# A transfer-bound mixture of softmaxes: loads and stores trade issuing engines, and one early unit is weighed in pairs

## The chip, the core and the metric

The kernel runs on one core of one Trainium2 chip. The metric is the device time of one execution in microseconds (us). The core's compute engines here are VectorE (DVE in the profile), ScalarE (ACT) and GpSimd (POOL); SyncE (SP) only issues transfers. Transfers started by SyncE and by ScalarE go through two queues (q1 and q10 in the profile) onto the same 16 transfer engines. All times compared below are fast runs, unless it is said otherwise.

## The reference

```python
batch, seq, vocab, num_heads = 32, 128, 4096, 4      # float32
prior_probs = softmax(prior, axis=-1)                # over the 4 heads
softmax     = softmax(logits, axis=-1)               # over the vocabulary
mixture     = np.sum(prior_probs[..., None] * softmax, axis=2)
```

The inputs are 268 MB of logits, the output is 67 MB. Both must cross the transfer engines once.

## The kernel before

The 4096 rows are cut into 32 **units** (U = 32) of 128 rows. One unit has four heads of 4096 columns, 8.39 MB, loaded into one of two halves of `ltile`. ScalarE takes the exponential of each head and its sum; VectorE takes a reciprocal, GpSimd multiplies it by the prior, and VectorE adds up the four weighted heads into one of two halves of `obuf`, which is stored. `only(ins, *keep)` states all that an instruction waits for.

```python
def load(u):                                   # SyncE issues
    ...
    ld = nc.sync.dma_start(out=ltile[:, u % 2, h:to], in_=lg[u // J, u % J, :, h:to, :])
    if u >= 2:
        only(ld, adds[u - 2, 0] if h == 0 else exps[u - 2, to - 1])
...
with tc.manual_schedule():
    load(0)
    nc.scalar.dma_start(out=pr, in_=pv)        # the prior
    load(1)
    ...
    for u in range(U):
        ...
        free = (stores[u - 2],) if bufd and u >= 2 else ()
        m = H if u < U - 4 else 2              # heads weighed in groups of m
        for h in range(H):
            if h == 2 and 0 < u < U - 3:
                store(u - 1, obuf[:, (u - 1) % 2], nc.scalar)   # ScalarE issues
            exp(h, *(free if m == H and h == H - 1 else ()))
            if (h + 1) % m:
                continue
            mul = weigh(g, m, ...)             # reciprocal, times prior
            for k in range(g, h + 1):
                add(k, mul, ...)               # VectorE; k = 0 writes, k > 0 adds
        if u + 2 < U:
            load(u + 2)
        ...                                    # the last stores, on SyncE
```

`exp(h)` of unit u waits for its load and, for h > 0, for `adds[u - 1, h]`, because the exponentials share one set of buffers. The fourth also waits for the store of unit u-2, since the weighings that follow overwrite its half of `obuf`.

The softmax here doesn't subtract the row's maximum and nothing guards it: scores larger than these inputs give would overflow.

Of the kernel before, what the change touches and what calls it, by code (L numbers as in the profile page):

```python
# [35 lines left out]
@with_exitstack  # L36
def kernel(
    ctx: ExitStack,
    tc: tile.TileContext,
    logits: bass.AP,  # L40
    prior: bass.AP,
    out: bass.AP,
):
    nc = tc.nc
    nc.at_finalize(early_transfers)
    B, S, H, V = logits.shape
    assert prior.shape == (B, S, H)
    assert out.shape == (B, S, V)
    P = 128
    J = 2  # L50
    R = P * J
    G = B * S // R
    U = G * J
    assert G * R == B * S and G <= 32 and H == 4

    lg = logits.rearrange("b s h v -> (b s) h v").rearrange("(g p j) h v -> g j p h v", p=P, j=J)
    ov = out.rearrange("b s v -> (b s) v").rearrange("(g p j) v -> g j p v", p=P, j=J)
    pv = prior.rearrange("b s h -> (b s) h").rearrange("(g r) h -> g r h", r=R)

    cpool = ctx.enter_context(tc.tile_pool(name="cpool", bufs=1))  # L60
    psum = ctx.enter_context(tc.tile_pool(name="psum", bufs=1, space=bass.MemoryType.PSUM))



    before = {}

    def only(ins, *keep):
        for k in keep:
            tc.add_manual_dep(
                ins.ins,  # L70
                k.ins.name,
                mybir.DependencyInfo(mybir.DependencyClass.Sync, mybir.DependencyReason.DATA),
                reason="all that this instruction waits for",
            )
        tc.declare_no_dep(
            ins.ins,
            group="loop",
            keep=[k.ins for k in keep] + before.get(ins.ins.engine, []),
            reason="covered by the waits that are kept",
        )  # L80
        tc.add_to_no_dep_group("loop", ins.ins)
        before[ins.ins.engine] = [ins.ins]
        return ins


    ltile = cpool.tile([P, 2, H, V], FP32, name="ltile")
    loads = {}
    exps = {}
    adds = {}
    stores = {}  # L90

    def load(u):
        if u == 0 or u >= U - 3:
            cuts = (0, 2, 3, 4) if u == U - 1 else (0, 2, 4)
        else:
            cuts = (0, H)
        for h, to in zip(cuts, cuts[1:]):
            ld = nc.sync.dma_start(  # L98
                out=ltile[:, u % 2, h:to], in_=lg[u // J, u % J, :, h:to, :]
            )  # L100


            if u >= 2:
                only(ld, adds[u - 2, 0] if h == 0 else exps[u - 2, to - 1])
            else:
                only(ld)
            for k in range(h, to):
                loads[u, k] = ld

    def store(u, acc, eng, lo=0, hi=V):  # L110
        st = eng.dma_start(out=ov[u // J, u % J, :, lo:hi], in_=acc[:, lo:hi])  # L111
        stores[u] = only(st, adds[u, H - 1])


    pr = cpool.tile([G, R, H], FP32, name="pr")
    pn = cpool.tile([32, H, R], FP32, name="pn")
    pmax = cpool.tile([G, R], FP32, name="pmax")
    pp = cpool.tile([P, J, H, 32], FP32, name="pp")


    dsum = cpool.tile([P, U, H], FP32, name="dsum")
    rden = cpool.tile([P, U, H], FP32, name="rden")
    coeff = cpool.tile([P, U, H], FP32, name="coeff")



    ebuf1 = cpool.tile([P, V], FP32, name="ebuf1")
    ebuf2 = psum.tile([P, V], FP32, name="ebuf2")
    ebuf3 = cpool.tile([P, V], FP32, name="ebuf3")
    obuf = cpool.tile([P, 2, V], FP32, name="obuf")  # L130

    with tc.manual_schedule():
        load(0)
        nc.scalar.dma_start(out=pr, in_=pv)
        load(1)
        nc.gpsimd.memset(pn, 0.0)  # L136
        nc.vector.reduce_max(pmax, pr, axis=AX.X)  # L137
        nc.vector.tensor_sub(pr, pr, pmax.unsqueeze(2).to_broadcast([G, R, H]))  # L138
        nc.scalar.activation(pr, pr, AF.Exp)  # L139
        nc.vector.reduce_sum(pmax, pr, axis=AX.X)  # L140
        nc.vector.reciprocal(pmax, pmax)  # L141
        nc.vector.tensor_mul(  # L142
            pn[0:G].rearrange("g h r -> g r h"), pr, pmax.unsqueeze(2).to_broadcast([G, R, H])
        )
        pq = pn.rearrange("g h (p j) -> g j h p", j=J)
        for t in range(P // 32):
            nc.vector.transpose(pp[32 * t : 32 * (t + 1)], pq[:, :, :, 32 * t : 32 * (t + 1)])  # L147

        for u in range(U):
            bufd = u < U - 2  # L150
            lt = ltile[:, u % 2]
            acc = obuf[:, u % 2] if bufd else lt[:, 0]
            es = (lt[:, 0], ebuf1, ebuf2, ebuf3) if bufd else [lt[:, h] for h in range(H)]
            ppu = pp[:, u % J, :, u // J]

            def exp(h, *keep):
                ex = nc.scalar.activation(  # L157
                    es[h], lt[:, h], AF.Exp, accum_out=dsum[:, u, h : h + 1]
                )
                keep = (loads[u, h],) + keep  # L160
                if bufd and h and u:
                    keep += (adds[u - 1, h],)
                exps[u, h] = only(ex, *keep)

            def weigh(h, n, *keep):
                rc = nc.vector.reciprocal(rden[:, u, h : h + n], dsum[:, u, h : h + n])  # L166
                only(rc, exps[u, h + n - 1])
                mul = nc.gpsimd.tensor_mul(  # L168
                    coeff[:, u, h : h + n], rden[:, u, h : h + n], ppu[:, h : h + n]
                )  # L170
                return only(mul, rc, *keep)

            def add(h, mul, lo=0, hi=V):
                if h == 0:
                    st = nc.vector.tensor_scalar(  # L175
                        out=acc[:, lo:hi], in0=es[h][:, lo:hi], scalar1=coeff[:, u, h : h + 1],
                        scalar2=None, op0=ALU.mult,
                    )
                    adds[u, h] = only(st, mul)
                else:  # L180
                    st = nc.vector.scalar_tensor_tensor(  # L181
                        out=acc[:, lo:hi], in0=es[h][:, lo:hi], scalar=coeff[:, u, h : h + 1],
                        in1=acc[:, lo:hi], op0=ALU.mult, op1=ALU.add,
                    )
                    adds[u, h] = only(st, mul, adds[u, h - 1])



            free = (stores[u - 2],) if bufd and u >= 2 else ()

            m = H if u < U - 4 else 2
            for h in range(H):
                if h == 2 and 0 < u < U - 3:
                    store(u - 1, obuf[:, (u - 1) % 2], nc.scalar)
                exp(h, *(free if m == H and h == H - 1 else ()))
                if (h + 1) % m:
                    continue
                g = h + 1 - m
                mul = weigh(g, m, *(free if m < H and g == 0 else ()))
                for k in range(g, h + 1):  # L200
                    n = 2 if u == U - 1 and k == H - 1 else 1
                    w = V // n
                    for c in range(n):
                        add(k, mul, c * w, (c + 1) * w)
                        if n > 1:
                            store(u, acc, nc.sync, c * w, (c + 1) * w)
            if u + 2 < U:
                load(u + 2)
            if u == U - 3:
                store(u - 1, obuf[:, (u - 1) % 2], nc.sync)  # L210
                store(u, acc, nc.sync)
            elif u == U - 2:
                store(u, acc, nc.sync)


# [28 lines left out]
```

## Time and profile before

| | kernel before |
|---|---|
| time, median (6 runs) | 780.93 us (780.84 to 781.11) |
| span in the profile | 779.3 us |
| VectorE, ScalarE busy | 67%, 60% |
| mean rate over the span | 431 GB/s |
| rate from 210 to 600 us | 434 GB/s |
| period of one unit in the steady part | 24.17 us |

How the transfers look is shown in the prediction. One more view is needed: the timeline of the same stretch from one store issue to the next. Columns of a timeline are start, duration, engine, line, instruction; in brackets the idle time before it and what ended it. (L111 issues a store, L157 is an exponential, L166 to L181 are the weighing.)

```profile
72.70 0.34 ACTq L111 DMA_DIRECT2D out_dram<-obuf  x1
73.09 3.59 ACT L157 ACTIVATE ebuf<-ltile 128x4096 f32<-128x4096 f32 x1 [1.06 <-DVE obuf L181]
...
76.71 3.60 ACT L157 ACTIVATE ebuf<-ltile 128x4096 f32<-128x4096 f32 x1
...
80.43 0.18 DVE L166 RECIPROCAL rden<-dsum 128x4 f32<-128x4 f32 x1 [7.76 <-ACT ebuf L157]
80.69 0.20 POOL L168 TENSOR_TENSOR coeff<-rden,pp 128x4 f32<-128x4 f32 x1 [23.96 <-DVE rden L166]
80.92 2.35 DVE L175 TENSOR_SCALAR obuf<-ltile,coeff 128x4096 f32<-128x4096 f32 x1 [0.31 <-POOL coeff L168]
83.31 13.53 DVE L181 SCALAR_TENSOR_TENSOR obuf<-ebuf,coeff,obuf 128x4096 f32<-128x4096 f32 x3
```

Follow it as a ring: the store is issued at 72.70, the third and fourth exponentials follow, then reciprocal, prior, one weighing of 2.35 and three that take 13.53 together, which end at 96.84; the next store is issued at 96.86. The ring is 96.86 - 72.70 = **24.16 us** long, and the transfers need 24.17 us for a unit.

### The profile page before, as it was taken

How to read it: one execution, taken by the hardware profiler on the slowest of the kernel's cores; microseconds unless marked ns; L12 is line 12 of the kernel's file. 1: busy time of each engine (PE TensorE's matmuls, PEld its weight loads, DVE VectorE, ACT ScalarE, POOL GpSimd, SP SyncE). 2: the span in 40 equal slices, each digit the busy share in tenths (PEclk: the TensorE clock that was granted, in tenths of full speed). 3: DMA queues.
4: the chain of work that ended last, by engine and by line, in shares of the span. 5: the costliest groups of instructions: out<-in, count | busy, mean ns of one | idle time of the engine just before them, and what ended most of it. 6: DMA issues, size and time to landing. Idle time of an engine off the chain costs nothing.

```text
span 779.3 us, 628 instructions
## 1 busy us (share of the span) xinstructions
DVE 521.0 (67%) x174; ACT 470.0 (60%) x258; POOL 8.3 (1%) x41
## 2 busy tenths in 40 slices
DVE  4447865568655686556875558755587555788986
ACT  4476555765557655577555675556755567557782
POOL 0000000000000000000000000000000000000000
DMA  9999999999999999999999999999999999999998
GB/s 407 457 417 397 474 407 417 444 455 434 404 468 401 460 420 416 458 443 418 417 468 407 454 407 468 420 415 447 415 459 417 459 402 464 410 427 431 434 429 379
DMA packets 10117, 335.65 MB, mean 431 GB/s; under 512 B 1137, under 2 KB 1137, under 8 KB 1153
## 3 DMA queue, kind: packets, MB, share of 16 engines
q1 hardware_dynamic: 6048, 276.83, 82.3%
q10 hardware_dynamic: 4064, 58.79, 17.6%
q14 instruction: 5, 0.03, 0.0%
HBM read 268.50 MB, written 67.11 MB: 431 GB/s over the span
## 4 chain that ended last, share of the span: by engine, by line
DVE 55%; ACT 26%; DMA 15%; issue 2%; ACTq 1%; POOL 1%; DVEq 0%; SPq 0%; POOLq 0%
DVE obuf L181 45%; ACT ebuf L157 24%; DMA ltile<-in_logits_dram 9%; DVE obuf L175 8%; DMA out_dram<-obuf 6%; ACT ltile L157 1%; ACTq L111 1%; DVE ltile L181 1%; POOL coeff L168 1%; DVE rden L166 1%; DVEq L239 0%; SPq L98 0%; POOLq L239 0%; POOLq L168 0%
## 5 line engine op out<-in xcount | busy, mean ns | idle before, releaser
L181 DVE SCALAR_TENSOR_TENSOR obuf<-ebuf,coeff,obuf 128x4096 f32<-128x4096 f32 x90 | 403.6, 4484 | 3.8 <-POOL coeff L168 0.6
L157 ACT ACTIVATE ebuf<-ltile 128x4096 f32<-128x4096 f32 x90 | 323.7, 3597 | 39.6 <-DVE obuf L181 32.2
L157 ACT ACTIVATE ltile<-ltile 128x4096 f32<-128x4096 f32 x38 | 137.3, 3614 | 247.6 <-DMA ltile<-in_logits_dram 247.6
L166 DVE RECIPROCAL rden<-dsum 128x4 f32<-128x4 f32 (+1 forms) x36 | 6.3, 175 | 230.3 <-ACT ebuf L157 227.5
L175 DVE TENSOR_SCALAR obuf<-ltile,coeff 128x4096 f32<-128x4096 f32 x30 | 70.6, 2353 | 10.3 <-POOL coeff L168 10.3
L181 DVE SCALAR_TENSOR_TENSOR ltile<-ltile,coeff 128x4096 f32<-128x4096 f32 (+1 forms) x7 | 27.0, 3874 | 0.8 <-POOL coeff L168 0.6
L157 ACT ACTIVATION_READ_ACCUMULATOR ebuf<-ltile 128x1 f32 x90 | 16.8, 186 | 0.0
L168 POOL TENSOR_TENSOR coeff<-rden,pp 128x4 f32<-128x4 f32 (+1 forms) x36 | 7.2, 200 | 755.3 <-DVE rden L166 745.2
L157 ACT ACTIVATION_READ_ACCUMULATOR ltile<-ltile 128x1 f32 x38 | 7.1, 186 | 0.0
L175 DVE TENSOR_SCALAR ltile<-ltile,coeff 128x4096 f32<-128x4096 f32 x2 | 4.7, 2353 | 0.6 <-POOL coeff L168 0.6
L137 DVE TENSOR_REDUCE pmax<-pr 16x256 f32<-16x1024 f32 x1 | 1.2, 1206 | 5.4 <-DMA pr<-in_prior_dram 5.4
L139 ACT ACTIVATE pr<-pr 16x1024 f32<-16x1024 f32 x1 | 1.1, 1055 | 5.7 <-DVE pr L138 5.7
L142 DVE TENSOR_TENSOR pn<-pr,pmax 16x1024 f32<-16x1024 f32 x1 | 1.9, 1925 | 0.1
L140 DVE TENSOR_REDUCE pmax<-pr 16x256 f32<-16x1024 f32 x1 | 1.2, 1208 | 1.1 <-ACT pr L139 1.1
L139 ACT ACT_TABLE_LOAD x1 | 1.3, 1283 | 0.9 <-PEq L228 0.9
L147 DVE STREAM_TRANSPOSE pp<-pn 32x256 f32<-32x256 f32 x4 | 1.7, 436 | 0.1
L141 DVE RECIPROCAL pmax<-pmax 16x256 f32<-16x256 f32 x1 | 1.7, 1741 | 0.0
L138 DVE TENSOR_TENSOR pr<-pr,pmax 16x1024 f32<-16x1024 f32 x1 | 1.2, 1211 | 0.0
L136 POOL MEMSET pn<- 32x1024 f32 x1 | 0.9, 941 | 0.5 <-POOLq L228 0.5
L228 POOL MEMSET const-bfloat16-1.0<- 128x1 bf16 x1 | 0.1, 107 | 0.0
L228 POOL MEMSET const-uint8-127<- 128x1 uint8 x1 | 0.1, 107 | 0.0
L228 POOL MEMSET const-float32-0.0<- 128x1 f32 x1 | 0.1, 103 | 0.2 <-issue 0.2
(1 smaller groups left out, 0.1 us busy)
## 6 DMA issues: line engine op xcount, KB each, us to landing
out_dram<-obuf ACTq DMA_DIRECT2D x28, 2048.0 KB, 28.1
ltile<-in_logits_dram SPq DMA_DIRECT2D x7, 4096.0 KB, 25.5
ltile<-in_logits_dram SPq DMA_DIRECT2D x2, 2048.0 KB, 30.9
out_dram<-obuf SPq DMA_DIRECT2D x2, 2048.0 KB, 33.9
out_dram<-ltile SPq DMA_DIRECT2D x1, 2048.0 KB, 17.2
out_dram<-ltile SPq DMA_DIRECT2D x2, 1024.0 KB, 4.8
ltile<-in_logits_dram SPq DMA_DIRECT2D x28, 29.6
pr<-in_prior_dram ACTq DMA_DIRECT2D x1, 64.0 KB, 5.2
```

The costliest lines, as they stand in the source:

```text
L111: st = eng.dma_start(out=ov[u // J, u % J, :, lo:hi], in_=acc[:, lo:hi])
L137: nc.vector.reduce_max(pmax, pr, axis=AX.X)
L138: nc.vector.tensor_sub(pr, pr, pmax.unsqueeze(2).to_broadcast([G, R, H]))
L139: nc.scalar.activation(pr, pr, AF.Exp)
L141: nc.vector.reciprocal(pmax, pmax)
L142: nc.vector.tensor_mul(pn[0:G].rearrange("g h r -> g r h"), pr, pmax.unsqueeze(2).to_broadcast([G, R, H]))
L147: nc.vector.transpose(pp[32 * t : 32 * (t + 1)], pq[:, :, :, 32 * t : 32 * (t + 1)])
L157: ex = nc.scalar.activation(es[h], lt[:, h], AF.Exp, accum_out=dsum[:, u, h : h + 1])
L166: rc = nc.vector.reciprocal(rden[:, u, h : h + n], dsum[:, u, h : h + n])
L168: mul = nc.gpsimd.tensor_mul(coeff[:, u, h : h + n], rden[:, u, h : h + n], ppu[:, h : h + n])
L175: st = nc.vector.tensor_scalar(out=acc[:, lo:hi], in0=es[h][:, lo:hi], scalar1=coeff[:, u, h : h + 1], scalar2=None, op0=ALU.mult,)
L181: st = nc.vector.scalar_tensor_tensor(out=acc[:, lo:hi], in0=es[h][:, lo:hi], scalar=coeff[:, u, h : h + 1], in1=acc[:, lo:hi], op0=ALU.mu ...
```

## The change

It swaps the issuing engines, so that ScalarE, which runs its program in order, no longer stands at a store until VectorE has finished a unit, and weighs unit 1 in two pairs of heads, so that VectorE starts it earlier. The last four stores go behind the last loads on the loads' queue, as they did before.

```diff
-            ld = nc.sync.dma_start(
+            ld = nc.scalar.dma_start(
...
-        nc.scalar.dma_start(out=pr, in_=pv)
+        nc.sync.dma_start(out=pr, in_=pv)
...
-            m = H if u < U - 4 else 2
+            m = 2 if u == 1 or u >= U - 4 else H
             for h in range(H):
                 if h == 2 and 0 < u < U - 3:
-                    store(u - 1, obuf[:, (u - 1) % 2], nc.scalar)
+                    store(u - 1, obuf[:, (u - 1) % 2], nc.sync)
+                if h == 2 and u == U - 1:
+                    store(u - 1, ltile[:, (u - 1) % 2, 0], nc.scalar)
...
-                            store(u, acc, nc.sync, c * w, (c + 1) * w)
+                            store(u, acc, nc.scalar, c * w, (c + 1) * w)
...
-            if u == U - 3:
-                store(u - 1, obuf[:, (u - 1) % 2], nc.sync)
-                store(u, acc, nc.sync)
-            elif u == U - 2:
-                store(u, acc, nc.sync)
+            if u == U - 2:
+                for k in (u - 2, u - 1):
+                    store(k, obuf[:, k % 2], nc.scalar)
```

## The prediction

> **What bounds the kernel now.** I read the page from the DMA rows downward, because the kernel does almost no arithmetic per byte: it reads 268 MB and writes 67 MB.
>
> ```profile
> DVE 521.0 (67%) x174; ACT 470.0 (60%) x258; POOL 8.3 (1%) x41
> ...
> DMA  9999999999999999999999999999999999999998
> ...
> DMA packets 10117, 335.65 MB, mean 431 GB/s; under 512 B 1137, under 2 KB 1137, under 8 KB 1153
> ...
> q1 hardware_dynamic: 6048, 276.83, 82.3%
> q10 hardware_dynamic: 4064, 58.79, 17.6%
> ```
>
> VectorE and ScalarE are each idle for a third of the span or more, while the transfer engines are at nine tenths in every slice but the last, and the two queues' shares add up to 99.9%. Queue 1 is SyncE's (all loads plus the four last stores: 268.4 + 4 x 2.1 = 276.8 MB), queue 10 is ScalarE's (28 stores of 2.1 MB and the prior). The chain that ended last is not what decides here: it is 55% VectorE and 26% ScalarE, because the compute loop is tuned to be just as long as the transfers. So I went to the waits, to see whether compute waits for data or data for compute.
>
> ```profile
> ACT ltile L157 <- DMA ltile<-in_logits_dram: 247.6, 32, 12.0
> DVE rden L166 <- ACT ebuf L157: 227.5, 30, 13.9
> ACT ebuf L157 <- DVE obuf L181: 32.2, 26, 1.9
> ...
> POOL coeff L168 <- DMA out_dram<-obuf: 10.0, 1, 10.0
> ```
>
> ScalarE waits 247.6 us for loads, about 8 us in each unit; VectorE then waits for ScalarE. The third line is ScalarE standing at the issue of a store: it sits between the second and third exponential of a unit until VectorE has finished the unit before, 32.2 us over 26 units, 1.24 us each. Next the timeline of one steady unit and of the next one's start:
>
> ```profile
> 88.32 3.62 ACT L157 ACTIVATE ltile<-ltile 128x4096 f32<-128x4096 f32 x1 [7.92 <-DMA ltile<-in_logits_dram]
> ...
> 96.86 0.34 ACTq L111 DMA_DIRECT2D out_dram<-obuf  x1
> 97.25 3.59 ACT L157 ACTIVATE ebuf<-ltile 128x4096 f32<-128x4096 f32 x1 [1.62 <-DVE obuf L181]
> ...
> 105.08 2.35 DVE L175 TENSOR_SCALAR obuf<-ltile,coeff 128x4096 f32<-128x4096 f32 x1 [0.32 <-POOL coeff L168]
> ```
>
> Unit 3's data is there at 88.32, unit 4's (from the same timeline) at 112.49, so the period is 24.17 us, and it repeats to 0.03 us in most of the 26 units. A unit moves 8.39 MB in and 2.10 MB out, 10.49 MB in 24.17 us = 433.8 GB/s. With stores absent the same rate appears: unit 1's load of 8.39 MB filled 22.39 to 41.73, 19.34 us, 433.7 GB/s. The rate is therefore the same with one or two queues in use, and the bound is that rate. The 335.65 MB of the kernel at 433.8 GB/s are 773.7 us. The remaining 5.6 us of the 779.3 us span are ends: the first 4.19 MB landed at 12.67 us where the rate alone would give 9.7 (about 3.0 us), the last 1 MB store took 4.8 us where the rate gives 2.4 (2.4 us). Some 0.7 us more was lost where two periods, 160.85 to 209.94, took 49.09 instead of 48.34 us; what disturbed them I cannot see.
>
> **What the Trainium skill says.** "DMA: Bandwidth & Descriptors", section "Where 436 GB/s comes from", puts the ceiling of a core's 16 ports at 435.2 GB/s; the 433.8 of the trace agrees, so no order of transfers should raise the steady rate. The same page, "Issuing engines are not separate DMA queues", says that transfers started by any engine run on the same 16 engines and that spreading them saves only issue time; the equal rates above agree. Its section "Queues, rings and completion order" says each engine takes turns between queues packet by packet. The mean packets here are 276.83 MB / 6048 = 45.8 KB and 58.79 MB / 4064 = 14.5 KB, semaphore packets included, and one store takes 28.1 us from issue to landing, where 2.1 MB alone would take 4.8: agrees with a turn of one 64 KB row of a load and one 16 KB row of a store, eight of each per engine and unit. "Perfetto Trace Analysis", section "DMA Optimizations", suggests one issuing engine for inputs and one for outputs; the kernel before does that already for nearly all transfers, so the change is a swap of the two.
>
> **The change part by part.**
>
> *Loads move to ScalarE's queue.* One load per unit, so one issue of about 0.34 us (the row of the store issue) replaces one store issue of 0.34 us: net zero in the loop. What moves is the place. The load of unit u+2 now stands after the fourth exponential of unit u and waits for VectorE's first weighing (reciprocal 0.18, GpSimd 0.20, gaps 0.3, weighing 2.35: about 3.1 us). ScalarE stands there 3.1 us which it otherwise would spend waiting for the next load: that wait is 7.9 to 8.4 us per unit. Nothing of it is on the path. In the kernel before the load is issued at 105.08 + 2.35 = 107.43, 5.1 us ahead of 112.49, when the load ahead of it lands; starting up costs about 3 us (the first load above), so the queue does not run dry.
>
> *Stores move to SyncE.* ScalarE loses the 1.24 us wait per unit. The third exponential can then start at about L + 7.3 instead of L + 8.9 (L is the landing of the unit). The fourth waits for the store of unit u-2 to land. In the kernel before that is exactly balanced: store issued 72.70, plus 28.1 is 100.8; the fourth exponential starts at 100.86. So most of the 1.6 us would merely turn into a wait for this store unless it lands earlier.
>
> *Unit 1 in pairs* is what makes it land earlier. VectorE is free at 46.14 and could start unit 1 after its second exponential (49.04) and not at 56.76. Two weighings (2.35 + 4.50) end at about 56.4, two more (9.0) at about 65.9, so store 1 is issued at 65.9 and not at 72.70, while store 0 is still moving (46.17 + 28.1 = 74.3). The store queue never goes empty, stores run some 2 us earlier from there on, and the fourth exponential is free again. Load 3 is issued at 56.2 instead of 59.1. All this is slack: the transfer engines are full either way. It could absorb part of the 0.7 us of disturbed periods: I count -0.4 us.
>
> *The tail.* The four last stores stood behind the last loads before as well; only the queue's name changes. Stores 28 and 29 now come after unit 30's exponentials (about 747) and not at 728 and 737, but the load of unit 31 keeps the queue busy till about 759. From 749.28, when the first pair of unit 31 has landed, two lengths must be compared. Transfers: 4.2 MB of loads and 8.4 MB of stores, 12.6 MB / 433.8 = 29.0 us. Compute: four exponentials to 763.79, then VectorE from 764.35 for 9.13 us, then 4.8 us for the last store: 778.3, also 29.0 us. ScalarE now issues store 30 between unit 31's second and third exponential; in the steady loop such an issue delays the next exponential by 0.39 us (96.86 to 97.25), of which 0.08 is the gap there anyway. So the compute tail grows by 0.3 us.
>
> *The head.* ScalarE's first issue is recorded at 0.13, SyncE's at 0.00: +0.1 us. The prior has 7 us of slack.
>
> Sum: 780.93 + 0.3 + 0.1 - 0.4 = 780.9, and I lean slightly to the good side because a looser store loop may save a little more at the join of head and loop: **780.6 us**.
>
> **The rivals.**
> 1. *ScalarE's new stand at the load issue starves the load queue.* For it: ScalarE runs in order, so a late store delays the fourth exponential, and that the load. Against it: 5.1 us lead against 3 us start-up, and stores waiting in the other queue would fill the engines. If each of 28 units lost 0.3 us, 789 us.
> 2. *The store wait was the real bound, and freeing it gains.* For it: the equality 100.8 and 100.86, and stores in the chain. Against it: queues at 99.9% and 433.8 GB/s with and without stores. At best the two disturbances and some of the ends go: 779 us.
> 3. *The tail gets worse:* stores 28 and 29 are issued about 19 and 10 us later and ScalarE carries more issues. If the load of unit 31 ended before they arrived, up to two stores' data, 2 x 4.8 us, would come after an idle gap; from the order of landings I see no gap. With half a store exposed: 783 us.
>
> **Range and chances.** The floor is 773.7 us plus about 5 us of ends plus 1.6 us between span and measured time, 780; below 778.9 I see no source. Above, rivals 1 and 3 reach 783 or so. Range 778.9 to 782.4. Over 2% either way is 15.6 us, which the bytes forbid on the fast side. Chances: faster 0.01, same 0.975, slower 0.015.
>
> **What would show it.** Right: queue 10 with 276.8 MB and queue 1 with 58.8, sum of shares above 99%; period still 24.17; ScalarE's 32.2 us wait for VectorE before the third exponential gone; store 1 issued near 66; the load of u+2 issued about 1.5 us earlier against L. Wrong: a period off 24.17 by 0.1 or more, a share below 98%, a growing wait of loads' readers, or a last store issued more than 1 us away from 773.5.

## The result and the profile after

| | before | after |
|---|---|---|
| time, median of 6 runs | 780.93 us (780.84 to 781.11) | 781.43 us (781.37 to 781.48) |
| span in the profile | 779.3 us | 779.5 us |
| rate from 210 to 600 us | 434 GB/s | 434 GB/s |
| unit 3 to unit 28, landing to landing | 605.16 us | 605.06 us |
| first load landed | 12.67 us | 12.25 us |
| last weighing ended | 773.5 us | 773.9 us |

The ratio is 1.0006, with a 95% interval of 0.9993 to 1.0019: the same. (A ratio is the mean time of one kernel's fast runs over that of the other's of the same rounds, so it is not quite the ratio of the medians above.) The 0.5 us between the medians repeats in these runs, but the interval does not tell it from nothing.

From the page of the kernel after, busy shares and queues:

```profile
DVE 521.0 (67%) x175; ACT 469.5 (60%) x258; POOL 8.5 (1%) x42
...
DMA  9999999999999999999999999999999999999998
...
q10 hardware_dynamic: 6048, 276.83, 82.2%
q1 hardware_dynamic: 4064, 58.79, 17.6%
```

The two queues have changed places, and the busy shares are the same. From the view of the waits (who waited for whom: total us, times, longest):

```profile
ACT ltile L157 <- DMA ltile<-in_logits_dram: 256.3, 32, 12.0
DVE rden L166 <- ACT ebuf L157: 228.9, 28, 16.7
ACT ebuf L157 <- DMA out_dram<-obuf: 27.5, 23, 1.5
...
POOL coeff L168 <- DMA out_dram<-obuf: 11.7, 1, 11.7
```

ScalarE's wait for VectorE (32.2 us in 26 waits) is gone. In its place stands a wait for stores to land, 27.5 us in 23 waits. The timeline shows where:

```profile
506.98 3.56 ACT L157 ACTIVATE ebuf<-ltile 128x4096 f32<-128x4096 f32 x1
...
511.88 3.62 ACT L157 ACTIVATE ebuf<-ltile 128x4096 f32<-128x4096 f32 x1 [1.21 <-DMA out_dram<-obuf]
...
516.12 2.35 DVE L175 TENSOR_SCALAR obuf<-ltile,coeff 128x4096 f32<-128x4096 f32 x1 [0.31 <-POOL coeff L168]
518.50 13.53 DVE L181 SCALAR_TENSOR_TENSOR obuf<-ebuf,coeff,obuf 128x4096 f32<-128x4096 f32 x3
518.56 0.33 ACTq L98 DMA_DIRECT2D ltile<-in_logits_dram  x1
523.94 3.62 ACT L157 ACTIVATE ltile<-ltile 128x4096 f32<-128x4096 f32 x1 [8.34 <-DMA ltile<-in_logits_dram]
```

The third exponential now runs without a wait, and the fourth stands 1.21 us for the store of two units ago. The load of the next unit but one goes out at 518.56, 5.4 us before 523.94, when the load ahead of it has landed; ScalarE still waits 8.34 us for that landing. The part headed 4, the chain that ended last by engine, first of before and then of after:

```profile
DVE 55%; ACT 26%; DMA 15%; issue 2%; ACTq 1%; POOL 1%; DVEq 0%; SPq 0%; POOLq 0%
```

```profile
DMA 60%; DVE 26%; ACT 10%; issue 2%; POOL 0%; DVEq 0%; ACTq 0%; POOLq 0%
```

The chain turned from compute to transfers, and the time stayed. That is what it looks like when one of two equal bounds is lifted; that there were two is argued here from the lengths 24.16 and 24.17 us, and shown by e6 and e12 below.

### The profile page after: what moved, and what is told of

It reads as the page before. It is cut to its first block, busy times and chain, and to the rows that moved or that the text cites. A ratio compares the mean times of both kernels' runs of the same rounds, so it can differ in the third digit from the quotient of the medians.

```text
span 779.5 us, 675 instructions
## 1 busy us (share of the span) xinstructions
DVE 521.0 (67%) x175; ACT 469.5 (60%) x258; POOL 8.5 (1%) x42
## 4 chain that ended last, share of the span: by engine, by line
DMA 60%; DVE 26%; ACT 10%; issue 2%; POOL 0%; DVEq 0%; ACTq 0%; POOLq 0%
DMA out_dram<-obuf 43%; DVE obuf L181 21%; DMA ltile<-in_logits_dram 17%; ACT ebuf L157 9%; DVE obuf L175 4%; ACT ltile L157 1%; DVE ltile L181 1%; POOL coeff L168 0%; DVE rden L166 0%; DVEq L241 0%; ACTq L98 0%; POOLq L241 0%; ACTq L157 0%
## 5 line engine op out<-in xcount | busy, mean ns | idle before, releaser
L157 ACT ACTIVATE ebuf<-ltile 128x4096 f32<-128x4096 f32 x90 | 323.3, 3593 | 34.4 <-DMA out_dram<-obuf 27.5
L157 ACT ACTIVATE ltile<-ltile 128x4096 f32<-128x4096 f32 x38 | 137.4, 3615 | 256.9 <-DMA ltile<-in_logits_dram 256.3
```

The lines of the kernel that those rows point to most:

```text
L157: ex = nc.scalar.activation(es[h], lt[:, h], AF.Exp, accum_out=dsum[:, u, h : h + 1])
```

## The experiments

**Theory** ("byte theory" in the expectations): the transfer rate of 434 GB/s sets the time of both kernels, and order matters only at the ends. **Rivals:** (a) a part of the change costs or gains at the head (the start), the join (where the head passes into the steady loop) or the tail (the end), and the parts cancel; (b) a compute ring or the store wait sets the period; (c) ScalarE's new duty, issuing loads, is close to harming them.

### Parts of the change alone

**e1: the changed kernel without pairs in unit 1.**

```diff
-            m = 2 if u == 1 or u >= U - 4 else H
+            m = 2 if u >= U - 4 else H
```

> The changed kernel with unit 1 weighed in one group of four again: the swap of the queues alone. Byte theory (the transfer engines' rate sets everything, order only matters at the ends): 781.4 us, within 0.3 of the changed kernel; the wait of the fourth exponential for a store stays about 1.2 us per unit, because the stores land as before. Rival (the pairs of unit 1 put the stores ahead of the loads and cost the 0.74 us seen between the landings of unit 1 and unit 3): 780.7 us, and unit 3 lands 46.6 us after unit 1 and not 47.3.

Measured: 781.32 us, ratio 1.0004 (0.9992 to 1.0017). Unit 3 landed 46.87 us after unit 1, against 47.33 in the changed kernel and 46.59 before; fourth exponentials wait 30.7 us for stores in all. The join moved as the rival said and the end did not move: unit 31's first pair landed at 749.60, against 749.47 with pairs. The rival falls.

**e2: the kernel before with pairs in unit 1.** The load of unit 3 needs a second wait, or it could overwrite heads still being read; in the changed kernel the load stands behind those exponentials in ScalarE's program, and it went out at 55.85, just after the last of them had ended (55.83).

```diff
-                only(ld, adds[u - 2, 0] if h == 0 else exps[u - 2, to - 1])
+                only(ld, *((exps[1, 3], adds[1, 0]) if u == 3 else (adds[u - 2, 0] if h == 0 else exps[u - 2, to - 1],)))
...
-            m = H if u < U - 4 else 2
+            m = 2 if u == 1 or u >= U - 4 else H
```

> The kernel before with unit 1 weighed in pairs and nothing else (the load of unit 3 must then wait for the fourth exponential as well). Byte theory: 780.9 us, within 0.3. Rival (pairs cost 0.7 us at the join of head and loop): 781.6 us, and unit 3 lands 47.3 us after unit 1 and not 46.6.

Measured: 781.38 us, ratio 1.0003 (0.9989 to 1.0017); 47.02 us from unit 1 to unit 3. Again a shift at the join which is gone at the end: unit 31's first pair landed at 749.28, exactly as before. One thing was not expected: ScalarE's wait for VectorE, 32.2 us before, is gone from this run's list too, and all its waits are for loads. The ring of 24.16 us is as long as a period, so a lag from the head is carried through the whole loop and so is a lead. Pairs in unit 1 put VectorE 7 us ahead once, and it stays ahead.

**e3: the changed kernel with the store of unit 30 and the two last half stores on SyncE.**

```diff
-                    store(u - 1, ltile[:, (u - 1) % 2, 0], nc.scalar)
+                    store(u - 1, ltile[:, (u - 1) % 2, 0], nc.sync)
...
-                            store(u, acc, nc.scalar, c * w, (c + 1) * w)
+                            store(u, acc, nc.sync, c * w, (c + 1) * w)
```

> The changed kernel with the store of unit 30 and the two half stores of unit 31 issued by SyncE. My theory: ScalarE's issue between the third-last and second-last exponential costs 0.3 us of the compute tail, so the last weighing ends 0.3 us sooner and the time is 781.1 us; if the 0.3 us by which measured time less span grew (1.93 against 1.63) also comes from ScalarE issuing the last store, 780.8. Rival (the tail is bound by the transfers, so an earlier issue only waits longer): 781.4 us with the last store taking longer from issue to landing.

Measured: 781.56 us, ratio 1.0007 (0.9994 to 1.0019). From the landing of unit 31's first pair (749.53) to the last weighing's end (773.74) there are now 24.21 us, against 24.47 in the changed kernel and 24.20 before. So ScalarE's issue did cost 0.26 us of compute, and removing it gained no time; the two half stores took 4.8 us to land (median), against 4.6. My theory of this part falls; the rival fits.

**e4: the kernel before with the prior's transfer not moved ahead of the start-up.**

```diff
-    for engine in (mybir.EngineType.SP, mybir.EngineType.Activation):
+    for engine in (mybir.EngineType.SP,):
```

> The kernel before with the prior's transfer issued in its ordinary place on ScalarE and not moved ahead of the start-up. In the changed kernel the prior went out first and the first load landed 0.42 us sooner (12.25 against 12.67). If the prior's rows between the load's rows are what costs 0.4 us, the first load lands at 12.6 still, since the prior still arrives in its midst; if the early issue itself is what collides, it lands at 12.2 and the time is 780.5 us. Byte theory for the whole: between 780.5 and 781.0 us.

Measured: 780.95 us, ratio 0.9998 (0.9986 to 1.0011). The first load landed at 12.66. The early issue of the prior is not what cost 0.42 us. The other cause named, the prior's rows among the load's, fits this number, but no run takes those rows away, so it is not shown. In all seven other kernels here that load from ScalarE's queue (e1, e3, e5, e7, e8, e9, e11) the first load landed at 12.17 to 12.30, in the five others that load from SyncE's (e2, e4, e6, e10, e12) at 12.63 to 12.77.

**e10: the kernel before with the last weighing and store in four pieces.**

```diff
-                    n = 2 if u == U - 1 and k == H - 1 else 1
+                    n = 4 if u == U - 1 and k == H - 1 else 1
```

> The kernel before with the last weighing and its store cut into four pieces and not two: the last store is 0.5 MB, 1.2 us less to move after the last weighing, which grows by two instructions' overheads, about 0.1 us. If the end is set by the compute tail: 780.0 us against 781.0. If the transfer engines are full until their end: 780.9 us, the last store waiting longer for its turn.

Measured: 781.41 us, ratio 1.0005 (0.9993 to 1.0018). The last pieces are half as large and still take 4.7 us to land, as the 1 MB pieces took 4.8. Like e3, this fits transfer engines that are busy nearly to the end: a smaller last piece only waits longer for its turn.

### What sets the period

**e6: the kernel before with VectorE weighing half of each row in units 0 to 29** (wrong result; `obuf` is filled once with zeros).

```diff
+                if bufd:
+                    hi = V // 2
```

> The kernel before with VectorE weighing only the left half of each row in units 0 to 29 (result wrong on purpose), all transfers the same. VectorE's work falls by about 240 us. Byte theory: 780.9 us, within 1 us. Rival (VectorE is 55% of the chain that ended last and sets the loop): tens of us faster, down to 720 us or less.

Measured: 781.10 us, ratio 1.0001 (0.9988 to 1.0015).

```profile
DVE 304.0 (39%) x175; ACT 466.7 (60%) x258; POOL 8.3 (1%) x41
```

217 us of VectorE's work gone (224 in the weighings, less 6.9 for filling `obuf`), no time gained. The compute ring shrank by about 7.5 us per unit (from 2.35 + 13.53 to 1.29 + 3 x 2.35), and the transfers alone hold 24.17 us. The rival, that VectorE's 55% of the chain sets the loop by itself, falls.

**e7: the changed kernel with no exponential waiting for a store** (weighings of units 0 to 29 write one buffer, stores read another; wrong).

```diff
-            acc = obuf[:, u % 2] if bufd else lt[:, 0]
+            acc = obuf[:, 0] if bufd else lt[:, 0]
...
-            free = (stores[u - 2],) if bufd and u >= 2 else ()
+            free = ()
...
-                    store(u - 1, obuf[:, (u - 1) % 2], nc.sync)
+                    store(u - 1, obuf[:, 1], nc.sync)
```

> The changed kernel with all weighings of units 0 to 29 writing one buffer and their stores reading another that nobody writes (result wrong on purpose), so that no exponential waits for a store; transfers the same. Byte theory: the 27.5 us of ScalarE waiting for stores vanish, the period stays 24.17 us, the time 781.4 us within 0.5. Rival (the store wait took the place of the VectorE wait and now sets the period): faster, up to 27 us, 754 us.

Measured: 781.77 us, ratio 1.0009 (0.9996 to 1.0023). From the waits:

```profile
ACT ltile L158 <- DMA ltile<-in_logits_dram: 287.0, 32, 12.0
```

The 27.5 us did not vanish from the engine, they turned into waits for loads (256.3 before, 287.0 now). The new wait costs nothing.

**e5, e11, e12: fewer bytes.** Only the left half of each row of units 0 to 29 is stored, 31.5 MB less. e5 does this to the changed kernel, e12 to the kernel before, e11 to e7's kernel, where no exponential waits for a store. Their outputs are wrong, which doesn't matter for the times.

```diff
     def store(u, acc, eng, lo=0, hi=V):
+        if u < U - 2:
+            hi = V // 2
```

> The changed kernel with only the left half of each row stored for units 0 to 29 (result wrong on purpose): 30 x 1.05 = 31.5 MB less to move, all engine work and its order the same. Byte theory: 31.5 MB / 433.8 GB/s = 72.5 us less, 709 us, queues' shares still above 99%. Rival (the loop of exponentials, weighings and store landings sets the 24.17 us, as the chain of waits suggests): less than half of that, above 745 us.

Measured: 722.63 us, ratio 0.9239 (0.9223 to 0.9255). Of the four runs in this median one, of 734.2 us, counts as slow and is left out of the ratio; the three fast ones have a median of 722.3 us (719.7 to 723.0). Closer to the bytes than to the rival, but 13 us short of them. The timeline shows one reason (L159 is the exponential, L98 the load's issue):

```profile
186.65 3.62 ACT L159 ACTIVATE ebuf<-ltile 128x4096 f32<-128x4096 f32 x1 [2.74 <-DMA out_dram<-obuf]
...
193.32 0.33 ACTq L98 DMA_DIRECT2D ltile<-in_logits_dram  x1
195.21 3.62 ACT L159 ACTIVATE ltile<-ltile 128x4096 f32<-128x4096 f32 x1 [4.85 <-DMA ltile<-in_logits_dram]
...
219.45 3.62 ACT L159 ACTIVATE ltile<-ltile 128x4096 f32<-128x4096 f32 x1 [8.91 <-DMA ltile<-in_logits_dram]
```

The store wait held the fourth exponential for 2.74 us, so the load went out only 1.9 us before the load ahead had landed, and its own landing came 24.24 us later; the bytes of such a unit need 21.75.

> Half stores as in the earlier run and, as in the run without store waits, weighings and stores on separate buffers (result wrong on purpose). The half-store run came to 722.6 us where the bytes gave 709. Two causes are proposed: the tail's 29.0 us of compute stands bare for 4.8 us because only 10.5 MB are left to move behind it, and in some units the wait for a store landing holds ScalarE, so that it issues the next load only 1.5 to 1.9 us before the load ahead lands, and the following unit comes 2 us late. If both are right, taking the wait away leaves only the first: 709 + 4.8 = 714 us and no period above 22.5 us in the loop. If the rate itself is lower with smaller rows, it stays at 722.

Measured: 713.56 us, ratio 0.9136 (0.9123 to 0.9150), no period above 22.12 us. Both causes hold, and the byte theory now gives the time to within 1 us: 781.4 - 72.5 for the bytes + 4.8 for the tail's bare compute is 713.7.

> The kernel before with the same half stores (result wrong on purpose). There the load's issue stands on SyncE, but it waits for a weighing that follows the same store wait. If the late loads come from the store wait, which both kernels have: 720 to 725 us as with the changed kernel. If they come from the load's place behind ScalarE's other work: about 714 us.

Measured: **776.03 us**, ratio 0.9936 (0.9919 to 0.9953). Neither expectation is near. Its timeline around one unit (L113 issues a store):

```profile
459.63 0.34 ACTq L113 DMA_DIRECT2D out_dram<-obuf  x1
460.02 3.59 ACT L159 ACTIVATE ebuf<-ltile 128x4096 f32<-128x4096 f32 x1 [5.58 <-DVE obuf L183]
...
469.63 3.62 ACT L159 ACTIVATE ltile<-ltile 128x4096 f32<-128x4096 f32 x1 [2.30 <-DMA ltile<-in_logits_dram]
...
483.80 0.34 ACTq L113 DMA_DIRECT2D out_dram<-obuf  x1
484.18 3.59 ACT L159 ACTIVATE ebuf<-ltile 128x4096 f32<-128x4096 f32 x1 [5.71 <-DVE obuf L183]
```

From issue to issue there are 483.80 - 459.63 = 24.17 us again, with a tenth of the bytes gone. ScalarE waits 5.6 us at each store's issue for VectorE, and only about 2 us for loads. This is the compute ring, alone: its wait for VectorE grew from 32.2 to 151.9 us, and the transfer rate between 210 and 600 us fell to 390 GB/s. So the kernel before does have a second bound at 24.17 us, and the changed kernel does not, since with the same bytes it ran at 722.3 us. **This is why lifting it gained nothing:** the change removed a true bound, beside which another of the same length was standing.

### How far the load's issue is from harm

**e8 and e9: the changed kernel with the loads of units 4 to 28 waiting for a later weighing.**

```diff
-                only(ld, adds[u - 2, 0] if h == 0 else exps[u - 2, to - 1])
+                only(ld, adds[u - 2, 2 if 4 <= u < U - 3 else 0] if h == 0 else exps[u - 2, to - 1])
```

(e9 has 1 in place of 2.)

> The changed kernel with the loads of units 4 to 28 waiting for VectorE's third weighing of the buffer's unit and not its first, 9.0 us later, so that ScalarE issues each load about 3 us after the load ahead has landed and not 5.4 us before. Here the load queue does run dry. Byte theory with stores filling the gap only partly (a store has 8 rows per engine, 4.8 us of full-rate work, against a gap of 3 + 3 us start-up): 1 to 6 us more per unit, 810 to 930 us. Rival (work waiting on the other queue always fills the engines): 781.4 us. Either way it measures how far the new place of the load was from harm.

Measured: 853.42 us, ratio 1.0924 (1.0909 to 1.0939), 72 us more than the changed kernel's 781.43, 2.9 us for each of 25 units; 387 GB/s from 210 to 600 us. The number lies in the range of the byte theory, but the trace shows another cause. First a line of the waits, then the timeline (L98 issues a load):

```profile
ACT ltile L157 <- DVE obuf L181: 210.6, 17, 12.4
```

```profile
497.99 0.33 ACTq L98 DMA_DIRECT2D ltile<-in_logits_dram  x1
498.37 3.62 ACT L157 ACTIVATE ltile<-ltile 128x4096 f32<-128x4096 f32 x1 [12.39 <-DVE obuf L181]
...
524.88 0.34 ACTq L98 DMA_DIRECT2D ltile<-in_logits_dram  x1
525.26 3.62 ACT L157 ACTIVATE ltile<-ltile 128x4096 f32<-128x4096 f32 x1 [12.38 <-DVE obuf L181]
```

ScalarE stands at the load's issue until VectorE's third weighing is done, and the next unit's first exponential stands behind that issue. Four exponentials, three weighings and the issue make a new compute ring of 525.26 - 498.37 = 26.89 us, with no transfer in it; in 17 units it is what ends ScalarE's wait. In the other units of the loop the load came last, with periods of 26.1 to 28.2 us. So this run shows mostly what a blocked issue does to the engine that carries it. Whether waiting stores would fill a gap between loads it does not show, since none was waiting: the load issued at 470.95 landed 26.4 us later, at 497.35, the store issued at 475.13 landed 23.4 us later, at 498.53, and the next store was issued only at 502.45.

> The changed kernel with the loads of units 4 to 28 waiting for VectorE's second weighing of the buffer's unit, 4.5 us later than in the changed kernel, about 0.9 us before the load ahead lands. Half of what the third weighing did. If a load needs about 3 us of lead (the start-up of the first load), 2 us per unit of queue time are lost, of which waiting stores fill some: 790 to 831 us. If 0.9 us of lead is enough: 781.4 us.

Measured: 792.67 us, ratio 1.0145 (1.0130 to 1.0161), 11.2 us or 0.45 us per unit more. In the steady part the load goes out about 2.5 us before the load ahead lands (507.54 and 510.00). Here ScalarE waits for each unit's load (298.4 us in 32 waits) and not for VectorE, so the transfers themselves are slower. The page of this run, rate and queues:

```profile
DMA packets 10116, 335.65 MB, mean 424 GB/s; under 512 B 1136, under 2 KB 1136, under 8 KB 1152
...
q10 hardware_dynamic: 6048, 276.83, 82.5%
q1 hardware_dynamic: 4064, 58.79, 17.4%
```

The shares still add up to 99.9%, yet the rate is 424 and not 431 GB/s. So the sum of shares that the prediction leaned on does not prove a full rate; the rate does. "Perfetto Trace Analysis", section "Identifying the Most-Contended Engine", says of transfers that occupancy over 16 engines misleads and that the throughput is to be judged; this run agrees. How the later issue lowers the rate is open. It is not a standstill where one load follows the other: with each packet's bytes spread evenly over its time, the trace gives 430 to 435 GB/s from 506 to 520 us, around the landing at 510.00, and 396 to 428 from 520 to 528.

## Why the prediction was right, and where its steps were not

- **The bound.** Right: 434 GB/s in both kernels over the same 390 us, 605.06 against 605.16 us over 25 units. e6, e7 and e11 carry it: less VectorE work and fewer waits changed nothing, fewer bytes changed the time by what they take. The parts that were added to it were partly wrong, and the lean to 780.6 went the wrong way.
- **The compute ring.** Only named in passing. Rival 2 looked for the second bound in the landing of stores ("the equality 100.8 and 100.86"); e7 shows that this wait is worth nothing, e12 that the ring through ScalarE's store issue was the second bound.
- **"The fourth exponential is free again."** This step failed. Store 1 was issued at 65.42, as predicted, but took 32.3 us to land since store 0 was still in the queue. The fourth exponential was free in units 2 to 4 only; from unit 5 on it waits 0.8 to 1.5 us. So of the signs that were named, the load issued 1.5 us earlier failed too: it went out 6.7 us ahead of the landing in unit 4 (106.11 and 112.82), but 5.4 in the steady part, against 5.1 before. Of the two sentences in the prediction, "would merely turn into a wait for this store" was the right one.
- **Absorbing disturbed periods (-0.4 us).** Not seen: periods of 24.49, 24.40 and 24.73 us stand in the changed kernel too. What disturbs them is open.
- **Head (+0.1 us).** The first load landed 0.42 us sooner, not 0.1 later. By unit 3 that lead was gone (47.33 us from unit 1 against 46.59), and e1 and e2 show that such shifts at the join don't reach the end.
- **Tail (+0.3 us).** The size is right, 24.47 against 24.20 us of compute, but in e3 and e10 time does not follow it. Still, the changed kernel stands at an edge here: from 770 to 774 us it moved 369 GB/s and the kernel before 406 (e1 354, e7 352, e3 379), so its engines stood partly empty before the last half stores came.
- **Stores 28 and 29** were expected at about 747 and went out at 739.8 (below). As foreseen, no gap opened: from 735 to 760 us 429 GB/s were moved, 425 before.
- **Rival 1** did not happen at a lead of 5.4 us. e9 puts the edge between 5.4 us, where nothing is lost, and 2.5 us. Its counter-argument, that waiting stores would fill the engines, was not tested by any run.

What makes up the 0.5 us between the medians stays open: single parts gave 781.3 to 781.6 us, and no verdict separates them from 781.0. The emptier engines of 770 to 774 us may be a part of it; that is not shown.

The line behind "below" is in the timeline of the kernel after, near the end:

```profile
739.75 3.62 ACT L157 ACTIVATE ltile<-ltile 128x4096 f32<-128x4096 f32 x1 [2.40 <-DMA ltile<-in_logits_dram]
739.76 0.84 ACTq L111 DMA_DIRECT2D out_dram<-obuf  x2
...
743.37 3.60 ACT L157 ACTIVATE ltile<-ltile 128x4096 f32<-128x4096 f32 x1
```

The two store issues come after the exponential of 743.37 in ScalarE's program and were sent 3.6 us before it started. ScalarE's issues need not wait until the exponentials ahead of them have run: an instruction that is already released queues up for the engine, and the issue passes by. What holds an issue here is a wait that is not yet met, its own or that of an instruction ahead. The load of unit 3 in the same kernel is such a case: the weighing that it waits for had ended at 51.48, but it went out at 55.85, and the chain of the profile names as its release the fourth exponential of unit 1, which ended at 55.83 and reads what the load overwrites.

## What to carry to other kernels

When the steady period equals bytes over rate, work out every other ring of waits in the loop as well, from one issue to the same issue a unit later: two rings of the same length look like one, and lifting one of them gains nothing until the other moves. To find such a pair, change one resource at a time by a lot, as the half stores did: the kernel whose time does not follow has the other bound. Measure the lead of each prefetch against the landing ahead of it, since some 3 us less of lead cost here 0.45 us per unit while the queues' shares still said full. And look at what stands behind an issue on a compute engine: in e8 it was the next unit's exponentials, and a ring of 26.89 us set the pace.

## What the Trainium skill lacked or had wrong

- "DMA: Bandwidth & Descriptors", section "Where 436 GB/s comes from", also says that for transfers between HBM and SBUF the HBM side, about 358 GB/s, binds. With one core running, 434 GB/s were sustained here over 390 us of mixed reads and writes; the page's port ceiling of 435.2 is the one that fits. The sentence lacks its condition, which the page gives under "Measured": about 358 GB/s is a core's part when both cores of an HBM domain stream.
- No page gives the lead that a load needs to keep its queue's rate. Here 5.4 us ahead of the previous landing lost nothing, about 2.5 us lost 0.45 us per unit (e9).
- No page explains why the first load landed at 12.17 to 12.30 us when ScalarE issued it and at 12.63 to 12.77 when SyncE did. The cause is open here too.
